# Values of all heads by seven products of quarters, in a stage of their own

## The chip, the cores and the metric

One core of one Trainium2 chip runs the whole kernel. The metric is the device time of one execution in microseconds. Three runs of the kernel before took 1961.91, 1963.91 and 1963.86 us, a median of 1963.86 us. Everything said of single instructions comes from one profiled execution of the same program.

## The reference

The model has two layers over 256 latent and 256 context tokens of width 2048. Layer 0 is bidirectional retention with 8 heads (q and k 256 wide, v and gate 512 wide per head), layer 1 is windowed attention. Cut to layer 0, on which the change bears:

```python
h = rms_norm(x) * (1 + scale) + shift            # scale, shift, gate from SiLU(c) @ ada_w
p = h @ w_in                                     # (512, 2048) @ (2048, 12288)
q, k, v, g = split(p)                            # per head: 256, 256, 512, 512 columns
q_l, k_l = rope_2d(q_l), rope_2d(k_l)            # latent tokens only, on a 4 x 64 grid
scores = (q @ k.T) / 16 * decay                  # gamma ** |i - j|, own gamma per direction
o = scores @ v                                   # latent tokens read context keys too
o = o * rsqrt(mean(o * o) + eps) * norm_gain
x = x + gate * ((o * silu(g)) @ w_out)
```

The modulation `SiLU(c) @ ada_w` gives shift, scale and gate for each layer and for two kinds of tokens, latent (c) and context (c_ctx). Layer 1's shift, scale and gate, and layer 0's gate, are needed only after the heads of layer 0. All matrices are float32.

## The kernel before

**Number format.** Every float32 operand of a large product is split into a high part (a rounded copy made by ScalarE, line 132 for weights, 116 for the rest) and a low part (the difference, made by VectorE, line 113). A product is then three matmuls, high x high, high x low, low x high: `mm3`, lines 137 to 142. A weight block is 256 rows by 512 columns, held as a tile of 128 x 1024 elements; `load_w` fetches it into one of three raw buffers over SP's queue and `split_w` makes the two parts, three buffers each.

**Start.** Tokens are loaded, normalised and modulated while TensorE already works on the queries and keys of heads 0 and 1 (`part0` and `part1`, lines 506 to 531). The products of head 0 stay in PSUM, those of head 1 are added up in SBUF (`qk1`).

**Head loop** (lines 899 to 925). Each head has three chunks of 512 weight columns: queries with keys, values, gate. A chunk is eight weight blocks. With tokens as the moving operand it is `gemm_ws`, with weights as the moving operand (values) `gemm_ts`; either way 4 x 16 calls of `mm3`, 192 matmuls of 512 columns. After each weight block a `hook` (line 727) issues a share of background work:

- one step of `sum_jobs` (line 311), which forms sums of quarters of the output projection in DRAM: a copy on ScalarE's queue, and an accumulating copy on POOL's queue held back by a tiny copy on POOL (`pin_t`);
- two steps of `ada_jobs` (line 694), the remaining modulation: a block of 128 x 512 of `adaB` is loaded and multiplied with the row of SiLU(c), once per kind of token, with a sum into one column (line 711, VectorE);
- one task of the head: moving queries and keys out with the rotation (`qk_evac`, line 739), a block of scores (`scores`, line 779), outputs, norm, and the parts of the gated branch (`parts`, line 836), whose sums POOL forms and which go to DRAM (`uB_d`) for the output projection.

The decay block of a head (`decays`, line 766) is two VectorE operations and a power of two on POOL (line 776); the rows come over ScalarE's queue.

**After the heads.** The output projection of layer 0 (lines 958 to 1154) is already computed by seven products of quarters: sums of weights come from DRAM (`wS_d`) or from VectorE (`comb`, line 974), and the accumulators are joined by ScalarE and VectorE (`merged`). Then layer 1 follows.

Instructions are written in program order, and a scheduler that knows dependencies and estimated durations sets the order on each engine; `tc.issue_after` holds instructions behind another one of the same engine. Each engine then works through its own order and waits on semaphores. A tile that shares its memory with an earlier one waits until that one is no longer used.

## Time and profile before

| what | value |
|---|---|
| three runs | 1961.91, 1963.91, 1963.86 us |
| span of the profiled execution, first to last instruction | 1959.6 us |
| its distance from the median of the runs | 4.3 us |
| TensorE busy | 1945.1 us, 99% |
| VectorE busy | 1350.5 us, 69% |
| ScalarE busy | 752.2 us, 38% |
| POOL busy | 481.6 us, 25% |
| bytes moved by DMA | 436.23 MB, mean 223 GB/s |
| start of the first chunk of the head loop, end of the last | about 148 and 1222 us |

An execution is described by the time from its first to its last instruction on the core. A row of instructions names line, engine, operation, output and inputs, count, busy time, the mean of one in nanoseconds, and the idle time ahead of it with what ended it. A row of a timeline gives the start, the duration and the instruction. The waits list for each engine who ended its idle time: total, times, longest. Matmuls overlap, so a busy TensorE is not yet one at its peak; distances between starts tell the rate.

### The profile page before, as it was taken

The numbers are of one execution on the slowest core, as the hardware profiler recorded it, in microseconds if no ns is written. First come the engines' busy times: TensorE is split into PE (matmuls) and PEld (weight loads), VectorE is DVE, ScalarE is ACT, GpSimd is POOL, SyncE is SP. The second block draws the span as 40 slices with busy tenths as digits, with TensorE's granted clock in tenths as the row PEclk, the third lists the DMA queues.
The fourth block names the chain that finished last, engine by engine and source line by source line (L and its number), as shares of the span: only waits on it lengthen the run. The fifth ranks groups of instructions, "written<-read, shape, count | busy, mean of one in ns | idle before, by whom it ended". The sixth has DMA issues, their size and how long they took to land.

```text
span 1959.6 us, 26859 instructions
## 1 busy us (share of the span) xinstructions
PE 1945.1 (99%) x9612; PEld 1612.6 (82%) x9612; DVE 1350.5 (69%) x2518; ACT 752.2 (38%) x1126; POOL 481.6 (25%) x389
## 2 busy tenths in 40 slices
PE   8999999999999999999999999999999999999999
PEld 4678888888888888888888888888888888888887
DVE  5566223788888888888565645877879746777764
ACT  4234223132222232232232334455555434766653
POOL 1218635525525526526300301100000100000000
PEclk9999999999999999999999999999999999999999
DMA  9965668898898998998755445677876324433365
GB/s 392 410 221 165 195 179 232 253 317 253 261 309 251 268 309 242 275 301 242 231 190 198 145 136 174 223 242 269 276 244 216 109 90 162 146 135 139 130 204 172
DMA packets 152039, 436.23 MB, mean 223 GB/s; under 512 B 18240, under 2 KB 37024, under 8 KB 146272
## 3 DMA queue, kind: packets, MB, share of 16 engines
q1 hardware_dynamic: 118976, 346.88, 50.6%
q0 software_dynamic: 10640, 34.87, 10.0%
q10 hardware_dynamic: 22288, 52.75, 7.8%
q8 instruction: 75, 1.23, 0.2%
q14 instruction: 60, 0.49, 0.1%
HBM read 416.04 MB, written 85.51 MB: 256 GB/s over the span
## 4 chain that ended last, share of the span: by engine, by line
PE 97%; DMA 1%; DVE 1%; issue 0%; ACT 0%; SPq 0%; DVEq 0%; ACTq 0%
PE acc L140 19%; PE acc L141 19%; PE acc L142 19%; PE acc L989 9%; PE acc L191 6%; PE acc L986 5%; PE acc L188 3%; PE pm L140 3%; PE pm L141 3%; PE pm L142 3%; PE acc L513 2%; PE pm L989 2%; PE pm L450 1%; PE pm L986 1%; PE pm L1307 1%; DMA rows<-gamT_d 1%
## 5 line engine op out<-in xcount | busy, mean ns | idle before, releaser
L132 ACT CAST wh<-wraw 128x1024 fp32r<-128x1024 f32 x415 | 435.2, 1052 | 848.5 <-PE acc L141 305.7
L113 DVE TENSOR_TENSOR wl<-wraw,wh 128x1024 fp32r<-128x1024 f32 x416 | 512.1, 1235 | 338.1 <-ACT wh L132 303.8
L140 PE MATMUL acc<-hT_h,wh 128*128 128x512 f32 x928 | 363.2, 391 | 1.0 <-DVE r_l L113 1.0
L141 PE MATMUL acc<-hl,wh 128*128 128x512 f32 x928 | 361.4, 389 | 0.0
L142 PE MATMUL acc<-hT_h,wl 128*128 128x512 f32 x928 | 361.2, 389 | 0.0
L711 DVE SCALAR_TENSOR_TENSOR ajunk<-abraw,crow 128x512 bf16<-128x512 f32 x448 | 344.2, 768 | 21.0 <-DMA abraw<-in_adaB 11.7
L142 PE MATMUL acc<-wh,hl 128*128 128x512 f32 x704 | 274.4, 390 | 0.0
L140 PE MATMUL acc<-wh,hT_h 128*128 128x512 f32 x576 | 224.7, 390 | 0.0
L141 PE MATMUL acc<-wl,hT_h 128*128 128x512 f32 x576 | 224.4, 390 | 0.0
L140 PEld LDWEIGHTS acc<-hT_h,wh 128*128 128x128 f32 x928 | 174.3, 188 | 38.0 <-DVE r_l L113 1.4
L142 PEld LDWEIGHTS acc<-hT_h,wl 128*128 128x128 f32 x928 | 174.2, 188 | 36.4
L141 PEld LDWEIGHTS acc<-hl,wh 128*128 128x128 f32 x928 | 174.4, 188 | 34.8
L241 POOL TENSOR_TENSOR rs<-ms,mhalf 128x4 f32<-128x4 f32 (+1 forms) x23 | 32.7, 1420 | 605.1 <-DVE ms L238 303.1
L776 POOL TENSOR_TENSOR dd<-two,dd 128x128 f32<-128x128 f32 x8 | 168.5, 21064 | 19.1 <-DVE dd L774 19.1
L142 PEld LDWEIGHTS acc<-wh,hl 128*128 128x128 f32 x704 | 132.2, 188 | 27.5
L322 POOL COPY pin_t<-wl 128x1 f32<-128x1 f32 x128 | 64.1, 500 | 317.5 <-DVE wl L113 313.2
L140 PEld LDWEIGHTS acc<-wh,hT_h 128*128 128x128 f32 x576 | 108.2, 188 | 23.1 <-issue 1.1
L141 PEld LDWEIGHTS acc<-wl,hT_h 128*128 128x128 f32 x576 | 108.2, 188 | 21.7
L324 POOL DMA_DIRECT2D wS_d<-in_wo x128 | 109.6, 872 | 11.2 <-issue 10.0
L843 POOL TENSOR_TENSOR ue<-sg 128x512 f32<-128x512 f32 x38 | 66.8, 1770 | 100.5 <-DVE sg L833 40.2
L829 POOL TENSOR_TENSOR ossq<-ossq,osq 128x512 f32<-128x512 f32 x24 | 35.3, 1470 | 185.7 <-ACT osq L823 185.0
L140 PE MATMUL acc<-wh,hl 128*128 128x512 f32 x192 | 75.4, 393 | 0.0
(282 smaller groups left out, 2915.1 us busy)
## 6 DMA issues: line engine op xcount, KB each, us to landing
wraw<-in_w SPq DMA_DIRECT2D x272, 512.0 KB, 4.2
abraw<-in_adaB SPq DMA_DIRECT2D x256, 256.0 KB, 5.5
wraw<-in_wo SPq DMA_DIRECT2D x80, 512.0 KB, 4.2
wS_d<-in_wo ACTq DMA_DIRECT2D x128, 256.0 KB, 5.2
wS_d<-in_wo POOLq DMA_DIRECT2D x128, 256.0 KB, 6.7
wraw<-wS_d SPq DMA_DIRECT2D x64, 512.0 KB, 4.5
araw<-in_adaS SPq DMA_DIRECT2D x28, 1024.0 KB, 11.5
wraw<-uB_d SPq DMA_DIRECT2D x20, 512.0 KB, 4.4
```

The costliest lines, as they stand in the source:

```text
L113: return nc.vector.tensor_tensor(out=out, in0=a, in1=hi.bitcast(F32), op=ALU.subtract)
L132: last_hi[0] = nc.scalar.copy(wh, raw).ins
L140: nc.tensor.matmul(ps, lhsT=ah, rhs=bh, start=start, stop=False, skip_group_check=skip)
L141: nc.tensor.matmul(ps, lhsT=ah, rhs=bl, start=False, stop=False, skip_group_check=skip)
L142: return nc.tensor.matmul(ps, lhsT=al, rhs=bh, start=False, stop=stop, skip_group_check=skip).ins
L191: nc.tensor.matmul(accs[j], lhsT=wk, rhs=h1(kb, s).rearrange("p a t -> p (a t)"), start=(kb == 0), stop=False)
L324: nc.gpsimd.dma_start(out=wS_d[i, r, q, x], in_=wo0_d[(*SUMS[i][1], r, q, x)], accum_op=ALU.add, max_dma_last_dim=4096)
L711: nc.vector.scalar_tensor_tensor(out=junk, in0=raw, scalar=1.0, in1=crow[:, t, q * 512:(q + 1) * 512], op0=ALU.mult, op1=ALU.mult, accum_o ...
L776: nc.gpsimd.tensor_tensor(out=dd, in0=two.to_broadcast([P, P]), in1=dd, op=ALU.pow)
L843: (nc.vector if now else nc.gpsimd).tensor_tensor(out=ue, in0=x, in1=y, op=op)
L986: last_pe[0] = nc.tensor.matmul(accs[j][:, 0:L], lhsT=wk, rhs=b[:, 0:L], start=False, stop=(kq == 3 and k == 3)).ins
L989: nc.tensor.matmul(accs[j], lhsT=wk, rhs=b, start=(kq == 0 and k == 0), stop=False)
```

## The change

The values of all heads leave the head loop. A stage ahead of it computes them in four pairs of heads. A pair is a product of 512 tokens by 2048 rows by 1024 columns, and each of the three sizes is halved: tokens into latent and context, rows into upper and lower half, columns into the two heads. Seven products of quarters (256 tokens, 1024 rows, 512 columns) replace eight. Sums of token quarters (`S`) are formed once, while TensorE computes the queries and keys of head 2; sums of weight quarters (`form`) are formed block by block; results are joined out of PSUM (`join`). All of these sums are VectorE's. Values go to DRAM (`v_d`) and are read back head by head (`v_load`). Queries and keys of heads 0 to 2 go through DRAM too (`qk_d`).

The order of the stage is written out in `VORDER`: each name is a product's accumulator group (X, Z, Y) and one of four row blocks; the position in the tuple says which sum of weights it takes.

```diff
+VORDER = ("X0 Z0 X1 Z1 X2 Z2 X3 Z3", "Y0 Z0 Y1 Z1 Y2 Z2 Z3 Y3", "X0 Y0 X1 Y1 X2 Y2 X3 Y3", "Y0 Y1 Y2 Y3")
...
-        t = strm.tile([P, 2, 512], F32, name="wraw", tag="wraw", bufs=3)
+        t = strm.tile([P, 2, 512], F32, name="wraw", tag="wraw", bufs=5)
...
+            for kp in range(4):
...
+                for j, x in enumerate(r):
+                    k, c = 2 * kp + 8 * (j % 2), half(j // 2)
+                    nc.vector.tensor_tensor(out=x, in0=hT_h[:, k:k + 2, c].bitcast(F32),
+                                            in1=hl[k // 2][:, :, c].bitcast(F32), op=ALU.add)
+                a11, a12, a21, a22 = r
+                for out, x, y, op in ((a22, a21, a22, ALU.add), (a21, a11, a21, ALU.subtract),
+                                      (a11, a22, a11, ALU.subtract), (a12, a12, a11, ALU.subtract)):
+                    nc.vector.tensor_tensor(out=out, in0=x, in1=y, op=op)
...
+                for i, x in enumerate((a22, a11, a21, a12)):
+                    split(S[i][:, ks, 0, :], S[i][:, ks, 1, :], x)
...
+            def form(self, g, m, kp):
+                raws, vt = self.raws, self.vt
+                if (g, m) == (0, "Z"):
+                    vt[kp] = ph.tile([P, 2, 512], F32, name="vt", tag=f"T{kp}")
+                    comb(vt[kp], raws[0, 12, kp], raws[0, 11, kp], ALU.subtract)
+                elif (g, m) == (1, "Y"):
+                    comb(vt[kp], raws[1, 22, kp], vt[kp], ALU.subtract)
+                elif (g, m) == (2, "Y"):
+                    comb(raws[2, 11, kp], vt[kp], raws[2, 11, kp], ALU.subtract)
+                    comb(vt[kp], raws[2, 21, kp], vt[kp], ALU.subtract)
...
+                for t in range(2):
+                    ts = slice(t * P, t * P + P)
+                    for k2 in range(2):
...
+                        mm3(acc[t], st, (wh[:, k2, :], wl[:, k2, :]),
+                            start=new and (kp, k2) == (0, 0), stop=last and k2 == 1, skip=True)
+                wide_hook(g)
+                if last:
+                    self.join(g, m)
...
+                if (g, m) == (0, "X"):
+                    self.q1 = self.tile("q1")
+                    each(lambda t, a: nc.scalar.copy(self.q1[:, t], a))
+                elif (g, m) == (0, "Z"):
+                    self.e = self.tile("e")
+                    each(lambda t, a: comb(self.e[:, t], a, self.q1[:, t], ALU.add))
...
+                elif (g, m) == (3, "Y"):
+                    each(lambda t, a: comb(self.q1[:, t], a, self.q1[:, t], ALU.add))
+                    self.store(1, 0, self.q1)
...
+        def wide_hook(g):
+            step_n[0] += 1
+            n = step_n[0]
+            if g != 2 and n % 2:
+                ada_step()
+            if n % 3 == 0:
+                next(sums, None)
...
+        for i in range(len(steps) + 3):
+            for what, back in (("load", 0), ("form", 1), ("parted", 2), ("mm", 3)):
```

The remaining modulation works on blocks of 128 x 1024 for 128 x 512; its raw blocks come through the same five buffers as the weights, and its steps are spread over the value stage (every other step, except in the third group) and the head loop (two per hook). What is left after the heads is issued at once (`ada_rest`). The sums of the output projection run at every third step of the value stage, at three of four hooks of the head loop, and for the rest at the hooks of the output projection itself.

```diff
+                for kb in range(KB):
+                    raw = load_raw(adaB_d[16 * part + kb, q].rearrange("p (a c) -> p a c", a=2))
+                    for t in range(ntk):
...
+                        nc.vector.scalar_tensor_tensor(
+                            out=junk, in0=flat, scalar=1.0, in1=crow[t],
+                            op0=ALU.mult, op1=ALU.mult, accum_out=asum[:, q, kb, t:t + 1])
```

The decay block is read from a table of powers in DRAM that is written once, each row shifted by one against the last. The rows of a head get a second buffer. The rotation's table shrinks to 4 row angles and 64 column angles, read with repetition.

```diff
+                nc.scalar.dma_start(out=skew_d.rearrange("h (r x) -> h r x", x=255),
+                                    in_=pow_d.unsqueeze(1).to_broadcast([H, P, 255]))
...
-            nc.vector.tensor_scalar(out=dd, in0=cst[:, C_T1:C_T1 + P], scalar1=lg2[:, h:h + 1],
-                                    scalar2=None, op0=ALU.mult)
-            nc.vector.scalar_tensor_tensor(out=dd, in0=cst[:, C_T2:C_T2 + P],
-                                           scalar=lg2[:, 8 + h:9 + h], in1=dd, op0=ALU.mult, op1=ALU.add)
-            nc.gpsimd.tensor_tensor(out=dd, in0=two.to_broadcast([P, P]), in1=dd, op=ALU.pow)
+            nc.scalar.dma_start(out=dd, in_=skew_d[h, 127:127 + P * 254].rearrange("(p x) -> p x", x=254)[:, 0:P])
```

In the head loop heads 0 to 2 keep only the gate chunk, with up to two tasks per hook; heads 3 to 6 have queries with keys and the gate; head 7 does its scores and its outputs inside its gate chunk, in an order written out (`plan`). The stores of the branch parts of heads 0 to 6 go from ScalarE's queue to POOL's. The gate's tile of a head is two tiles, in different memory for even and odd heads. The scratch memory for POOL's DMA descriptors is set to 4096 bytes.

```diff
         def hook():
+            state["n"] += 1
+            n = state["n"]
+            if n % 4 != 0:
+                next(sums, None)
+            if n > 2:
+                ada_step(2)
+            pump(rate[0])
...
-                    (nc.gpsimd if h == H - 2 else nc.scalar).dma_start(out=uB_d[m, h], in_=ue)
+                    (nc.scalar if h == H - 1 else nc.gpsimd).dma_start(out=uB_d[m, h], in_=ue)
...
+                if h:
+                    tasks.extend([e[0], outs[0], e[1], outs[1], nothing, v[0], outs[2], v[1], sc[0], sc[1],
+                                  outs[3], outs[4], sc[2], sc[3]])
...
+        plan = ([lambda: v_load(H - 1, 1), lambda: v_load(H - 1, 0)] + score_tasks(H - 1)[:1],
+                score_tasks(H - 1)[1:], outs[:1], outs[1:2] + [(M1, 2), (M1, 3)],
+                [(M1, 4), (M1, 5), (M1, 6), (M4, 0), (M4, 1)], outs[2:3] + [(M4, 5), (M4, 6), (M4, 2), (M4, 3)],
+                outs[3:] + [(M4, 4), (M1, 0), (M1, 1)])
```

374 lines of the change are left out of this document (237 added, 137 removed).

## The prediction

> **What bounds the kernel now.** I read the page's shares first, then who made TensorE wait, then stretches of the span, and last the single instructions.
>
> ```profile
> span 1959.6 us, 26859 instructions
> PE 1945.1 (99%) x9612; PEld 1612.6 (82%) x9612; DVE 1350.5 (69%) x2518; ACT 752.2 (38%) x1126; POOL 481.6 (25%) x389
> ```
>
> TensorE is busy 99% of the span. A matmul's end is modelled, so that share alone could hide gaps. The waits of TensorE say how many there are:
>
> ```profile
> PE pm L405 <- DMA x<-in_xT: 5.0, 1, 5.0
> PE acc L513 <- ACT hT_h L274: 3.0, 2, 1.8
> PE acc L140 <- DVE r_l L113: 1.0, 1, 1.0
> PE pm L450 <- DMA araw<-in_adaS: 0.5, 1, 0.5
> ```
>
> The four longest add up to 9.5 us, and all but 1.0 us of it lies at the start, ahead of the head loop. So the head loop has no idle that a change could win back; it gets shorter only if TensorE has less to do. What one matmul costs there is the distance between starts:
>
> ```profile
> 804.42 0.39 PE L140 MATMUL acc<-hT_h,wh 128*128 128x512 f32 x1
> 804.65 0.39 PE L141 MATMUL acc<-hl,wh 128*128 128x512 f32 x1
> 804.87 0.39 PE L142 MATMUL acc<-hT_h,wl 128*128 128x512 f32 x1
> 805.10 0.39 PE L140 MATMUL acc<-hT_h,wh 128*128 128x512 f32 x1
> 805.33 0.39 PE L141 MATMUL acc<-hl,wh 128*128 128x512 f32 x1
> ```
>
> Four distances take 0.91 us, so 0.2275 us each; the 0.39 us is latency.
>
> Who could take over as the bound is read from stretches of the span (columns: length, busy time of PE, PEld, DVE, ACT, POOL, granted clock, DMA share, GB/s):
>
> ```profile
> 400.00:900.00 500.00, 499.02 (x2269) 414.16 (x2268) 418.43 (x952) 137.54 (x200) 210.73 (x196) 1.00 0.91 278
> 1222.00:1310.00 88.00, 88.00 (x505) 76.94 (x504) 69.87 (x77) 43.31 (x59) 6.00 (x3) 1.00 0.68 227
> 1310.00:1534.00 224.00, 224.00 (x1286) 196.71 (x1285) 183.95 (x280) 123.78 (x180) 1.49 (x1) 1.00 0.71 242
> ```
>
> In the head loop VectorE is 84% busy and the DMA engines 91%, and TensorE does not stop. In the output projection of the first layer (the other two rows) VectorE is 79% and 82% busy, again with TensorE full. The granted clock is 1.00.
>
> **TensorE's term.** Before, the values of two heads cost 2 x 4 token blocks x 16 row blocks x 3 passes = 384 matmuls of 512 columns. After, a pair takes 28 steps (seven products of four steps each) of 2 token blocks x 2 row blocks x 3 passes: 336. Over four pairs that is 1344 for 1536, all of the 128x512 shape quoted: 192 fewer, 192 x 0.2275 = 43.7 us less. Queries and keys of head 2 are moved ahead, not removed; the transpose of the modulation row is moved to the start; scores and outputs keep their matmuls.
>
> [...]
>
> **What VectorE gets.** Prices are start to start, since an instruction's reported end overlaps the next start:
>
> ```profile
> 1249.88 3.49 DVE L113 TENSOR_TENSOR wl<-wraw,wh 128x1024 fp32r<-128x1024 f32 x3
> 1260.61 1.28 DVE L113 TENSOR_TENSOR hT_h<-wraw,hT_h 128x512 fp32r<-128x512 f32 x2
> 553.00 0.69 DVE L711 SCALAR_TENSOR_TENSOR ajunk<-abraw,crow 128x512 bf16<-128x512 f32 x1
> 553.61 0.08 DVE L711 DVE_READ_ACCUMULATOR ajunk<-abraw,crow 128x1 f32 x1
> 553.73 0.69 DVE L711 SCALAR_TENSOR_TENSOR ajunk<-abraw,crow 128x512 bf16<-128x512 f32 x1
> L113 DVE TENSOR_TENSOR wl<-wraw,wh 128x1024 fp32r<-128x1024 f32 x416 | 512.1, 1235 | 338.1 <-ACT wh L132 303.8
> ```
>
> Three wide subtractions in a row span 3.49 us, the last lasting 1.22: 1.135 us apart, for a mean duration of 1.235. Two narrow ones span 1.28 us: 0.60 apart. So 512 more elements cost 0.535 us. A narrow modulation sum takes 0.73 us start to start; the wide one, which the trace does not show, lies between 1.135 (a wide sum without the accumulator) and 1.46 (two narrow ones). I take 0.73 + 0.535 = 1.27, the nearest by shape. The 224 wide sums then take 284 us where 448 narrow ones took 327.
>
> By stage, VectorE against TensorE:
>
> 1. Chunk of head 2's queries and keys, 192 matmuls, 43.7 us. VectorE: 8 weight splits x 1.135 = 9.1; the four sums of token quarters, 32 adds and 16 split subtractions of 512 elements x 0.60 = 28.8; four ends of the start, 2.4. Together 40.3, 92%. What is late here is first needed a few products later, so I cost it at nothing; without that cover the loss is the excess alone.
> 2. Value stage, per pair 336 x 0.2275 = 76.4 us. VectorE: 28 splits and 16 weight sums, 44 x 1.135 = 49.9; ten joins out of the accumulators x 0.60 = 6.0; ten steps of modulation, 12.3 us (32 of 33 hold a sum). Together 68.2, 89%. ScalarE's 28 casts (row below) take 29 us.
> 3. Heads 0 to 2: one gate chunk each, 43.7 us, and 12.5 us of scores and outputs (36 matmuls of 512 columns, and 36 of 256 at 0.12 us, rows below): 56. VectorE: 8 splits 9.1, 16 modulation steps 19.7, and the head's own work (rotations, value splits, scores, outputs). That is worked out from the row 400 to 900: a head took 3 x 43.7 + 12.5 = 143.6 us, so 3.48 heads and 83.6 weight blocks lie in it, each with a split and four narrow sums, 1.135 + 4 x 0.73 = 4.06 us; 418.4 - 339.4 = 79 us are left, 22.7 a head, and 22 without the decay block. Together 51 us, 91%. Head 0 has no outputs to finish yet, 5 us less on both engines: 46 of 48, 96%.
> 4. Heads 3 to 6: two chunks, 100 us of TensorE; VectorE 18 + 39 + 22 = 79.
>
> ```profile
> L132 ACT CAST wh<-wraw 128x1024 fp32r<-128x1024 f32 x415 | 435.2, 1052 | 848.5 <-PE acc L141 305.7
> ...
> 783.21 0.28 PE L140 MATMUL pm<-r_h 128*128 128x256 f32 x1
> 783.33 0.28 PE L141 MATMUL pm<-r_l,r_h 128*128 128x256 f32 x1
> ```
>
> **Queues.** Moving the values costs transfers: 80 weight loads for 64, 16 stores of sums on ScalarE's queue and 16 loads back on SP, queries and keys of three heads out (ScalarE, and four on POOL) and in (SP), and the skewed rows: some 32 MB more. What the queues give:
>
> ```profile
> q1 hardware_dynamic: 118976, 346.88, 50.6%
> q0 software_dynamic: 10640, 34.87, 10.0%
> q10 hardware_dynamic: 22288, 52.75, 7.8%
> ```
>
> 346.88 MB in 50.6% of the span is 350 GB/s while busy; the accumulating queue 34.87 MB in 10.0%, 178 GB/s. In the value stage (306 us): 41.9 MB of weights, 10.5 of modulation, 8.4 of stores and 9.7 of copies at 350, 9.7 of accumulation at 178: 201 + 55 = 256 us, 84%. Heads 0 to 2, by the same prices for their 15 MB, come to about 50 of 56 us. Both lie under the 0.91 of the stretch 400 to 900, in which TensorE never waited. So the cost is nothing while the loads lead; if they do not, rival D.
>
> **Decays.** The power on POOL and its two VectorE operations go (L776: 8 x 21 us on POOL, and 0.6 us per head on VectorE), one small load on ScalarE's queue comes; the second buffer for the rows lets them come a head earlier:
>
> ```profile
> L776 POOL TENSOR_TENSOR dd<-two,dd 128x128 f32<-128x128 f32 x8 | 168.5, 21064 | 19.1 <-DVE dd L774 19.1
> DVE d L792 <- DMA rows<-gamT_d: 36.7, 7, 10.4
> ```
>
> These 36.7 us are VectorE's, none of it reached TensorE: worth nothing by itself, though it leaves VectorE freer. POOL takes on the stores of the branch parts (256 KB each, 4.1 us to landing, row under rival D); it was busy 25%.
>
> **New waits.** Each pair has five joins on VectorE, each waiting for the last matmul of a product. Behind a join in VectorE's order stand the sums and the split of the next steps, for which TensorE waits. The output projection has the same pattern: a step of 8 + 8 matmuls (about 2.8 us against 2.73 here), combined weights, joins, and it loses nothing at 79% to 82%. Not shown is 89%. A stall per join lies between 0 and, if all that may stand ahead comes late, 3.2 us (rival C). I take 0.2 us for each of the 20 joins, near the row of the same pattern: 4 us. The handover to head 0, whose tiles take the value stage's memory, and the last head, whose scores now share one chunk with its outputs (VectorE about 30 of 56 us), lie under a chunk each; bounds 0 and the landing of one 512 KB load (4.2 us, row under rival D) each; I take 1 each.
>
> **Sum**, against the profiled execution: 1959.6 - 43.7 + 4 + 2 = 1921.9 us of span. The runs shown have a median of 1963.86, 4.3 us above the span; so 1926 us.
>
> **Rivals.**
> B: VectorE becomes the bound where it is fullest. For: 89% to 96% is above anything in the trace. Against: it is less than full. Price: if the 16% that VectorE idled from 400 to 900 us are forced idle (waits for casts, transfers, products), the value stage needs 273 / 0.84 = 325 us instead of 306, the chunk ahead 48 for 44, heads 0 to 2 148 / 0.84 = 176 for 160: +39 us in full, 1959. At half that idle almost nothing is left (297, 44 and 161 us). I price it between, at 1942.
> C, slower: VectorE and TensorE go in lockstep at the joins. Two joins (1.2), two weight sums (2.27), a modulation sum (1.27) and the next split (1.135) stand in a row, 5.9 us, while TensorE has one step of 2.73 us prepared: 3.2 us lost at each of 20 joins, 64 us, 1984. It decides the sign from 2.2 us per join on. Against: weights can be split two steps ahead in three buffers, and the output projection shows no such loss. [...]
> D: modulation and weights share five raw buffers on SP's queue; a modulation block held by a late VectorE keeps weights from being fetched. The landing takes 4.2 us:
>
> ```profile
> wraw<-in_w SPq DMA_DIRECT2D x272, 512.0 KB, 4.2
> uB_d<-ue POOLq DMA_DIRECT2D x5, 256.0 KB, 4.1
> ```
>
> With a load late by half of that in one of four steps of the value stage it is 28 x 2.1 = 59 us at worst, and a fourth of that, 15 us, as its price: 1941. Against: five buffers are some five steps of lead, 13 us.
> E: the saved matmuls do nothing, because another limit sets the time: 1964. Against: the waits above.
>
> **How the numbers follow.** Forecast A (1918 to 1933) 0.62, B 0.18, C 0.08, D 0.08, E 0.04. The time is that of A, 1926. The low end is the fastest run less the whole saving, 1961.9 - 43.7 = 1918, and 2 us for unknown gains: 1916. The high end takes in most of B and D: 1956. About 0.2% (4 us) is what a measurement of this kernel can tell from no change. Faster: A, and nearly all of B and D: 0.87; same: E and the edge of B: 0.04; slower: C and the tail of D: 0.09.
>
> **What would show it.** Right: the value stage lasts 306 to 315 us with TensorE without waits and VectorE near 90%; the wide sum near 1.27 us apart; heads 0 to 2 some 56 us each; TensorE's matmuls 192 fewer. Wrong: TensorE's waits naming VectorE's weight split (B or C; in C right behind the joins) or raw loads (D) for more than 15 us in all.

## The result and the profile after

The changed kernel is slower: 2018.93 us (median of four, 2012.8 to 2021.72) against 1962.88 us before on the same chip (median of four), a ratio of 1.0282 with a 95% interval of 1.0265 to 1.03. The forecast was 1926. Of all the executions in this document one, of e15 below, took 6793.87 us; it is left out of that kernel's figures.

The head of the page of the changed kernel answers to the rows of before:

```profile
span 2011.0 us, 25977 instructions
PE 1935.6 (96%) x9420; PEld 1590.3 (79%) x9420; DVE 1487.8 (74%) x2250; ACT 820.9 (41%) x1214; POOL 374.6 (19%) x415
...
q1 hardware_dynamic: 106944, 371.59, 53.4%
q0 software_dynamic: 13360, 43.79, 11.1%
q10 hardware_dynamic: 23368, 56.95, 8.4%
```

TensorE has 9420 matmuls for 9612, so the 192 are gone. But its share fell from 99% to 96%, and VectorE, at 74%, is nowhere near full over the span. The longest of TensorE's waits (total, times, longest) say what came in:

```profile
PE acc L144 <- DVE t L947: 16.4, 6, 4.0
PE acc L145 <- DVE wl L114: 9.3, 8, 2.0
PE acc L146 <- DVE wl L114: 7.3, 3, 4.8
PE pm L145 <- DVE wl L114: 7.1, 7, 1.7
PE pm L1181 <- DVE x L1187: 5.8, 3, 3.1
PE pm L416 <- DMA x<-in_xT: 5.5, 1, 5.5
PE acc L144 <- ACT wh L136: 5.1, 3, 3.8
PE acc L1181 <- ACT wh L136: 4.3, 2, 2.8
PE pm L253 <- POOL ossq L1014: 3.2, 3, 1.6
```

All waits of TensorE, these and eight smaller groups, add up to 70.9 us; before they were 10.2. L947 is the rotation in a head's evacuation, L114 the split of a weight, L1187 a join of the output projection; the wait for `x` lies at the start, as before.

The waits are only half of it. This is TensorE's timeline around the first long pause:

```profile
160.58 0.39 PE L145 MATMUL acc<-hl,wh 128*128 128x512 f32 x1
165.79 0.79 PE L146 MATMUL acc<-hT_h,wl 128*128 128x512 f32 x1 [4.81 <-DVE wl L114]
166.38 0.63 PE L144 MATMUL acc<-hT_h,wh 128*128 128x512 f32 x1
166.80 0.63 PE L145 MATMUL acc<-hl,wh 128*128 128x512 f32 x1
...
171.07 0.56 PE L146 MATMUL acc<-hT_h,wl 128*128 128x512 f32 x1
171.47 0.39 PE L144 MATMUL acc<-hT_h,wh 128*128 128x512 f32 x1
```

Behind the pause the starts lie about 0.4275 us apart instead of 0.2275. From 165.79 to 171.07 there are 12 distances in 5.28 us where 2.73 would do: the pause of 4.81 us cost another 2.55 us. The granted clock of the changed kernel is 1.00 from 161.18 to 164.59, a stretch without a matmul, 0.50 from there to 171.42 and 1.00 behind, so the wide distances lie where half the clock is granted (shorter pauses: last section). The mean granted clock over the span is 0.986, against 0.999 before. As an estimate, if TensorE had had work all the time, that costs 2011.0 x 0.014 - 1959.6 x 0.001 = 26 us.

So the 51.4 us between the two spans are: -43.7 (matmuls saved) + 60.7 (more waiting) + 26 (clock) + 8 that neither view explains.

By stretches (length; busy time of PE, PEld, DVE, ACT, POOL; granted clock, DMA share, GB/s), cut at the start of the chunk of head 2's queries and keys, at the last copy of its results, at the last join of the values and at the last gate product of head 7:

```profile
148.00:201.00 53.00, 47.40 (x196) 38.12 (x195) 39.65 (x58) 20.34 (x29) 1.08 (x2) 0.94 0.40 129
201.00:530.00 329.00, 312.21 (x1344) 250.97 (x1343) 271.33 (x292) 127.90 (x130) 47.74 (x70) 0.99 0.81 245
530.00:1262.50 732.50, 703.38 (x3204) 582.37 (x3204) 563.83 (x915) 236.99 (x383) 239.99 (x246) 0.98 0.83 261
1262.50:2011.00 748.50, 733.87 (x3939) 628.35 (x3938) 531.16 (x808) 386.66 (x595) 68.37 (x83) 1.00 0.60 193
```

Without any waiting these would be 43.7, 306, 681 and 737 us: the first two from the prediction; the last is what lay behind the heads before (from 1222.8 to 1959.6); the third is the rest, 1959.6 - 43.7 - 148 - 43.7 - 306 - 736.8. The chunk lost 9 us, the value stage 23, the heads 51, the tail 12. All tables below use this cut.

### The profile page after: what moved, and what is told of

It is laid out like the page before. It is cut to its first block, busy times and chain, and to the rows that moved or that the text cites. A ratio compares the mean times of both kernels' runs of the same rounds, so it can differ in the third digit from the quotient of the medians.

```text
span 2011.0 us, 25977 instructions
## 1 busy us (share of the span) xinstructions
PE 1935.6 (96%) x9420; PEld 1590.3 (79%) x9420; DVE 1487.8 (74%) x2250; ACT 820.9 (41%) x1214; POOL 374.6 (19%) x415
## 3 DMA queue, kind: packets, MB, share of 16 engines
q1 hardware_dynamic: 106944, 371.59, 53.4%
## 5 line engine op out<-in xcount | busy, mean ns | idle before, releaser
L114 DVE TENSOR_TENSOR wl<-wraw,wh 128x1024 fp32r<-128x1024 f32 x416 | 512.4, 1237 | 248.0 <-ACT wh L136 236.8
L144 PE MATMUL acc<-hT_h,wh 128*128 128x512 f32 x928 | 371.4, 400 | 22.8 <-DVE t L947 16.4
L326 POOL COPY pin_t<-wl 128x1 f32<-128x1 f32 x128 | 91.0, 711 | 702.7 <-DVE wl L114 702.7
L678 DVE SCALAR_TENSOR_TENSOR wraw<-wraw,crow 128x1024 f32<-128x1024 f32 x128 | 169.3, 1329 | 14.2 <-DMA crow<-crow_d 11.3
L678 DVE SCALAR_TENSOR_TENSOR ajunk<-wraw,crow 128x1024 bf16<-128x1024 f32 x96 | 128.0, 1333 | 4.2 <-issue 3.0
L146 PE MATMUL acc<-wh,hl 128*128 128x512 f32 x320 | 125.3, 392 | 0.0
L136 ACT CAST wh<-vt 128x1024 fp32r<-128x1024 f32 x48 | 50.6, 1054 | 80.3 <-PE acc L146 35.6
L145 PE MATMUL acc<-wl,hT_h 128*128 128x512 f32 x192 | 75.8, 395 | 3.4 <-DVE wl L114 3.4
L144 PE MATMUL acc<-wh,hl 128*128 128x512 f32 x192 | 75.4, 393 | 0.0
L144 PE MATMUL pm<-r_h 128*128 128x512 f32 (+1 forms) x216 | 74.4, 344 | 1.0 <-DVE sg L1010 1.0
L144 PE MATMUL acc<-wh,hT_h 128*128 128x512 f32 x192 | 75.0, 392 | 0.2 <-ACT wh L136 0.2
L145 PE MATMUL acc<-wl,hl 128*128 128x512 f32 x192 | 74.9, 390 | 0.0
L145 PE MATMUL pm<-r_l,r_h 128*128 128x512 f32 (+1 forms) x216 | 74.1, 343 | 0.4 <-DVE r_l L114 0.4
## 6 DMA issues: line engine op xcount, KB each, us to landing
araw<-in_adaS SPq DMA_DIRECT2D x28, 1024.0 KB, 11.4
```

Of the source, the lines that this page charges most:

```text
L114: return nc.vector.tensor_tensor(out=out, in0=a, in1=hi.bitcast(F32), op=ALU.subtract)
L136: last_hi[0] = nc.scalar.copy(wh, raw).ins
L144: nc.tensor.matmul(ps, lhsT=ah, rhs=bh, start=start, stop=False, skip_group_check=skip)
L145: nc.tensor.matmul(ps, lhsT=ah, rhs=bl, start=False, stop=False, skip_group_check=skip)
L146: return nc.tensor.matmul(ps, lhsT=al, rhs=bh, start=False, stop=stop, skip_group_check=skip).ins
L326: pin = nc.gpsimd.tensor_copy(pin_t, last_wl[0][:, 0, 0:1].bitcast(F32)).ins
```

## The experiments

Where the text calls a kernel "the base", it is the changed kernel with six raw buffers and the values' reads behind the evacuation (e9). A "raw buffer" holds a block as it was loaded, ahead of its split; an "accumulating transfer" adds what it moves to what lies in DRAM. Code is shown shortened; some of the remarks behind # stand here alone. The executions of one of these kernels scatter more than those of before: four of the changed kernel span 9 us, four of e17 (below) 9 us, seven of e15 18 us. So single runs under some 20 us apart are told apart by their stages and waits, not by their totals. The stages are those of one profiled execution; it took 2012.8 us of the changed kernel, the fastest of its four, and 1982.2 of e15, the slowest of its seven.

An edit also lets the scheduler order the rest anew. By the traces, 253 instructions of VectorE lie in the value stage; against the changed kernel some 11% of them come in another order in e3, 19% in e4, 22% in e1 and 43% in e2. So these four runs show what an edit did together with its new order.

| kernel | time | chunk | values | heads | tail |
|---|---|---|---|---|---|
| forecast (1926 with 6 us of waits; the stages without any) | 1926 | 43.7 | 306 | 681 | 737 |
| changed | 2018.9 | 53.0 | 329.0 | 732.5 | 748.5 |
| e1 modulation without loads in the value stage | 2007.1 | 53.0 | 323.2 | 731.8 | 749.3 |
| e2 no weight sums in the value stage | 2016.1 | 51.8 | 310.2 | 744.0 | 760.0 |
| e3 modulation loads without sums | 2040.2 | 51.6 | 346.7 | 737.1 | 755.0 |
| e4 six raw buffers | 1987.2 | 50.0 | 317.6 | 715.7 | 754.1 |
| e5 values behind the evacuation | 1998.7 | 51.8 | 332.7 | 715.8 | 748.7 |
| e6 weight sums in the heads | 2020.2 | 53.4 | 330.0 | 748.1 | 738.9 |
| e7 later token sums, later head 0 | 2024.9 | 49.9 | 335.9 | 735.8 | 753.6 |
| e8 e4 to e7 together | 1984.1 | 47.3 | 322.0 | 725.4 | 739.5 |
| e9 base: e4 and e5 | 1976.7 | 52.3 | 317.4 | 705.5 | 751.7 |
| e10 base, modulation buffers apart | 2019.1 | 53.1 | 326.6 | 738.5 | 751.2 |
| e12 base, store through ScalarE | 1978.8 | 49.6 | 322.8 | 707.2 | 749.4 |
| e13 base, head 0 one step later | 1980.1 | 51.9 | 318.3 | 704.7 | 755.4 |
| e14 base, weight sums in the chunk | 1975.9 | 55.7 | 323.3 | 707.8 | 739.2 |
| e15 base, e12 to e14 | 1976.4 | 50.6 | 330.8 | 711.6 | 739.4 |
| e16 base, no accumulating transfer | 1942.2 | 51.6 | 307.9 | 694.4 | 738.1 |
| e17 base, weight sums spread | 1980.0 | 52.2 | 322.8 | 714.9 | 738.7 |
| e18 base, plain transfer instead | 1950.3 | 51.4 | 317.6 | 692.4 | 739.1 |

**Is VectorE full, or are the weights late?** (rivals B and D of the prediction: e1 to e4)

In e1 the value stage's modulation sums read a resident row instead of a raw block, so their loads are left out; in e3 the loads stay and the sums run over 8 columns; in e2 only the place of the weight sums changes.

```diff
 e1: +  flat = crow[t] if own else raw.rearrange("p a c -> p (a c)")     # own: value stage, no load
 e2: -            if n % 3 == 0:
     -                next(sums, None)                                   # value stage
     -            if n % 4 != 0:
     +            # every step of the head loop
                      next(sums, None)
 e3: +  cols = slice(0, 8 if in_values[0] else 1024)
     +  out=junk[:, cols], in0=flat[:, cols], scalar=1.0, in1=crow[t][:, cols],
 e4: -  t = strm.tile([P, 2, 512], F32, name="wraw", tag="wraw", bufs=5)
     +  t = strm.tile([P, 2, 512], F32, name="wraw", tag="wraw", bufs=6)
```

> Kernel after, but in the value stage the modulation sums multiply the resident row of SiLU(c) with itself: the same 40 wide sums on VectorE, none of their 20 loads through the raw buffers (a part of the modulation is left out). In the kernel after the value stage lasts 329 us (201 to 530) for 306 us of matmuls, with 17 us of TensorE's idle. Theory ring (weights come late because modulation shares the five raw buffers and holds them): stage about 312 us, TensorE idle under 5 us. Rival VectorE full: stage unchanged within 4 us. Rival DMA engines full: a little shorter, 320 to 326 us, as 10.5 of 80 MB go.

> Kernel after, but none of the sums of the output projection's weights in the value stage; they run at every hook of the head loop and the rest at the hooks of the output projection. 19 of 80 MB leave the value stage, and POOL's small copies that hold the weight buffers. Theory ring: stage about 325 us, little changed. Rival DMA engines full: stage about 312 us. Rival VectorE full: unchanged at 329 us. In all theories the time after the heads grows by some us, since 35 steps instead of 22 are left for it.

> Kernel after, but in the value stage each modulation sum works on 8 columns instead of 1024 (a part of the modulation is left out): loads and raw buffers as before, VectorE has 40 x 1.1 = 44 us less to do in the stage. Theory VectorE full: stage about 312 us. Theory ring: buffers are let go a little earlier, stage 322 to 329 us. DMA engines full: 329 us.

> Kernel after with six raw buffers for five (one buffer of the first modulation strips is given up for it, and most of the scratch memory of POOL's descriptors). Theory ring: value stage 318 to 324 us, and head loop shorter too, in all 10 to 30 us less. VectorE full or DMA engines full: value stage unchanged within 4 us.

e3 takes work off VectorE and the value stage gets longer, 346.7 for 329.0. None of the theories had that, and why it got longer stays open; it speaks against VectorE's load as the limit, and e16 below settles it. Taking traffic away shortens the stage: 323.2 without the modulation loads, 310.2 without the weight sums, both as the rival of full DMA engines had it (in e2 the time comes back in the heads and the tail). A sixth buffer shortens it to 317.6 with all the work in place and the heads by 17 us, as the theory of the ring, the shared buffers, had it. The sixth buffer's room comes from one buffer less for the modulation strips of the start (six for seven) and 1280 bytes of GpSimd's descriptor memory for 4096; these two sizes were not run alone. e10 has them too and gains nothing, which speaks against them but does not exclude them.

ScalarE's waits for a weight block, in its casts, show the lateness: in the kernel before,

```profile
ACT wh L132 <- DMA wraw<-in_w: 5.9, 2, 4.4
```

and in the changed kernel, with the waits of VectorE's sums of weights and of ScalarE's casts of values read back:

```profile
ACT wh L136 <- DMA wraw<-in_w: 116.7, 29, 9.5
ACT r_h L120 <- DMA wraw<-v_d: 55.5, 10, 10.1
DVE vt L117 <- DMA wraw<-in_w: 26.3, 17, 3.3
DVE wraw L117 <- DMA wraw<-in_w: 18.7, 12, 3.7
```

The median landing of a weight block hardly moved, 4.5 us for 4.2. What grew is how often a block isn't there when its cast is next. This row is a sign and no price: in e5 it is longer still, 135.2 us, with a shorter time, and in e16, the fastest version, 60.0 us are left.

**The values read back** (e5)

ScalarE's timeline in head 4 of the changed kernel, in the middle of the evacuation of queries and keys:

```profile
862.57 0.37 ACT L120 CAST r_h<-acc 128x256 fp32r<-128x256 f32 x1 [0.49 <-PE acc L146]
869.69 0.62 ACT L120 CAST r_h<-wraw 128x512 fp32r<-128x512 f32 x1 [6.75 <-DMA wraw<-v_d]
870.21 0.36 ACT L120 CAST r_h<-acc 128x256 fp32r<-128x256 f32 x1
```

A cast of the values waits 6.75 us for its load, the rest of the evacuation stands behind it, and TensorE, which needs the accumulators, pauses:

```profile
871.95 0.77 PE L144 MATMUL acc<-hT_h,wh 128*128 128x512 f32 x1 [3.98 <-DVE t L947]
```

```diff
+        def v_behind(h, i):
+            with tc.issue_after(last_ev[0]), tc.issue_after(last_ec[0]):   # last sum and last cast of the evacuation
+                v_load(h, i)
-                tasks.extend([lambda i=i: v_load(h, i) for i in (1, 0)] + score_tasks(h))
+                tasks.extend([lambda i=i: v_behind(h, i) for i in (1, 0)] + score_tasks(h))
```

> The changed kernel with one order altered: the two reads of a later head's values (v_load, heads 3 to 7), with their split on ScalarE and VectorE, are ordered behind the evacuation of that head's queries and keys, instead of wherever the planner finds room. Theory W (values read back are a new wait in front of the evacuation): in the changed kernel ScalarE's cast of the values waited 6.75 us at 869.69 for its transfer, the rest of the evacuation stood behind it, and TensorE paused for 2.4 to 4.0 us in each of heads 3 to 7 and ran slower right after; this run takes the waits of accumulator tiles for t (16.4 us in all) to near nothing and shortens the head stage from 732.5 to 710-722 us; the total falls to 1998-2010. Theory F (VectorE is full in the head stage, so a pause moves elsewhere): the head stage stays within 4 us of 732 and the waits come back at the scores that now get their values later.

As theory W had it in the stage: 732.5 to 715.8 us, total 1998.73. The value stage keeps its order of instructions, and nearly its length (332.7). The waits for t fell by half only, from 16.4 to 9.0 us, and not to near nothing: the rest stands behind a cast for a weight that came late, in the middle of the same evacuation (ScalarE's timeline of e5):

```profile
869.40 0.37 ACT L122 CAST r_h<-acc 128x256 fp32r<-128x256 f32 x1
872.26 1.04 ACT L138 CAST wh<-wraw 128x1024 fp32r<-128x1024 f32 x1 [2.49 <-DMA wraw<-in_w]
```

**The moved weight sums, the token sums, head 0** (e6, e7, e8)

In the tail three of TensorE's waits, 5.8 us, are for joins of the output projection (L1187 above), whose loads now share the transfers with the sums.

```diff
 e6: -            if n % 4 != 0:
     -                next(sums, None)
     +            next(sums, None)
     -                    next(sums, None)                              # in the output projection
 e7: +        stats, skip = stat_jobs(), [2]                            # first two calls do nothing
     -                    tasks.extend([lambda: (e[0](), e[1]()), lambda: (v[0](), v[1]()), nothing] + sc)
     +                    tasks.extend([nothing] * 5 + [e[0], e[1], nothing, v[0], v[1]] + sc)
```

> The changed kernel with the sums of weights for the output projection and the feed-forward part (sum_jobs) placed at every hook of the head loop instead of three of four, what is left finished ahead of the output projection, and none inside the output projection's own loop. Theory S (the sums that the change moved into the output projection cost there): a copy on GpSimd waited 6.85 us there, ScalarE's cast waited 8.81 us behind it, and TensorE's pauses of 1 to 3 us add up to some 10 us with what the slower clock adds; this run brings the tail from 748.5 to 735-742 us and costs the head stage up to 6 us. Theory N (the tail is longer for another reason, its own loads): the tail stays within 3 us of 748.5, and the head stage grows by the moved sums.

> The changed kernel with two places of its order altered: the token-quarter sums in the chunk of head 2's q and k begin two steps later (the last of them are finished right behind the chunk), and the reads of queries, keys and values of head 0 come at least two hooks later. Theory Q (in each place a load's wait stands on VectorE or ScalarE ahead of the split of a weight): the chunk falls from 53.0 to 44-48 us, and the pauses of 3.80 and 1.87 us in head 0 go, 4 to 8 us of the head stage; the total falls to 2000-2008. Theory R (the additions themselves are what delays the split, whatever they wait for): the chunk stays at 51-54 us or the time comes back at the start of the value stage, whose 329 us then grow.

> Six raw-weight buffers instead of five, together with the three edits of the runs beside it (values read behind the evacuation, sums of weights in the head loop alone, later token sums and later head 0). If the losses are separate and each has the cause named, they add up: chunk 44-48, value stage 312-320, head stage 695-715, tail 735-745, total 1935-1960, below the kernel before. If they share one limit (bytes per second or VectorE's total work), the total stays above 1970, and the value and head stages hold what the edits took from the others.

e6: the tail falls to 738.9 as theory S had it, and no pause for a join is left in it (one of 3.57 us at its start, for a weight's cast, stays); but the head stage takes 15.6 us more, where the theory allowed 6, so nothing is won. e7: the chunk falls by 3 us only, and a pause of 4.88 us appears at the start of the value stage; head 0's pause comes back later, 5.67 us at its outputs. That is theory R's outcome. e8, with everything, has each stage better than the changed kernel but the total at 1984, above the 1970 at which the losses were to be called one shared limit.

**Separate or shared buffers; the wide sums alone** (e9, e10, e11)

e11 also takes over the compact rotation table, which makes the room, and issues the sums one by one, where the kernel before issued them in pairs.

```diff
 e10: +    def load_m(src):                                              # modulation blocks
      +        t = strm.tile([P, 2, 512], F32, name="mraw", tag="mraw", bufs=2)
      -    wraw ... bufs=6
      +    wraw ... bufs=4
 e11 (on the kernel before):
      -                    for q in range(4):
      +                    for q in range(2):
      +                        raw = (top["pool"] if q else pb).tile([P, 2, 512], ...)
      -  in1=crow[:, t, q * 512:(q + 1) * 512]
      +  in1=crow[:, t, q * 1024:(q + 1) * 1024]
```

> Six shared raw buffers together with the values' reads behind the evacuation, and nothing else altered. Alone these two took 31.8 us and 20.2 us off the changed kernel. Theory A (two separate causes): they add up, 1963-1975, with the head stage at 700-708 us. Theory B (both relieve the same lateness of loads in the head stage): the second adds less than 8 us, 1979-1987, head stage 712-716 us.

> The same six buffers and the same order of the values' reads as the run beside it, but the buffers are split: four for the weights and the values read back, two of their own for the wide modulation loads, as the kernel before keeps the two apart. Theory O (the weights' loads are late because on SyncE's queue they stand behind a modulation load that waits for VectorE to finish an earlier sum of the same ring; in the changed kernel those waits come to 211.9 us): SyncE's queue waits for the wide sums fall, TensorE's waits for weights in the value and head stages fall below 15 us, and the time is 10-25 us under the run beside it. Theory L (what matters is how many buffers are ahead of the weights, not who holds them): with four in place of six for the weights the value stage goes back to 325-332 us and the time is 5-25 us above it.

> The kernel before with one part of the change alone: modulation sums of 1024 columns instead of 512, from two buffers of 4 KB that the modulation keeps for itself (four of 2 KB before), and the rotation's compact table, which makes the room for them. Values, decays and every other order stay as before. By the rows, a 512 sum takes 0.74 us start to start and a wide one 1.33 us with its read of the sum, so VectorE saves some 0.15 us in each pair, 230 x 0.15 = 35 us of busy time off the path. Theory P (the wide sums are harmless by themselves): within 0.4% of the kernel before, 1956-1968. Theory Q (a sum of 1.33 us, or a modulation load of 512 KB, in front of a weight's split is long enough to stop TensorE by itself): 10 to 30 us slower, with TensorE's waits naming VectorE's weight split in heads 1 to 6.

e9: 1976.7, between the two theories, with the head stage at 705.5 as theory A had it; the second edit still takes 10 us off the stage, so the causes are mostly separate. e10 was a miss for both theories, but for the value stage, which comes out at L's length (326.6): the time goes back to 2019.1, 42 us above e9 and beyond what L allowed, although the casts wait for weights less than in any other variant of the changed kernel, 21.5 us. The lateness has moved to the modulation: VectorE now stands in front of the splits waiting for its blocks (waits of VectorE in e10):

```profile
DVE ajunk L685 <- DMA mraw<-in_adaB: 43.1, 19, 5.6
DVE mraw L685 <- DMA mraw<-in_adaB: 29.4, 19, 3.1
```

In the base, with six buffers for all, these waits are 3.3 us together. e11 points the same way with the kernel before: 1971.13 against 1961.9, ratio 1.0041 (1.0027 to 1.0056), between the two theories. From two buffers of their own the wide sums, with the rest of that edit, cost 8 us; VectorE waits 65 us for their blocks, where the narrow sums waited 11.7, and TensorE pauses three times in the head loop, 6.9 us together.

**The three places that were left** (e12 to e15, on the base)

```diff
 e12: -            nc.gpsimd.dma_start(out=qk_d[1, :, j], in_=ends[j])
      +            nc.scalar.dma_start(out=qk_d[1, :, j], in_=ends[j])
 e13: -                    tasks.extend([lambda: (e[0](), e[1]()), lambda: (v[0](), v[1]()), nothing] + sc)
      +                    tasks.extend([nothing, nothing, e[0], e[1], v[0], v[1], nothing] + sc)   # two a step
 e14: +            next(sums, None)
      +            next(sums, None)                                      # each step of head 2's chunk
      -                    next(sums, None)                              # in the output projection
```

> Base: six shared raw buffers and the values read behind the evacuation (1976.72). Altered alone: the four stores of head 1's finished q and k go out through ScalarE's queue instead of GpSimd's. In the changed kernel VectorE's first token sum waited 8.18 us at the start of the chunk of head 2's q and k, for memory that the closed pool still stored from (stores landing 15.4 us after their issue). Theory H (that store is what it waits for): the wait falls by 5 us or more, the chunk from 52.3 to 44-47 us, the total to 1969-1973. Theory K (it waits for the other stores, of head 0's q and k or the decays): the chunk stays at 51-53 us and the total at 1975-1979.

> Same base. Altered alone: in head 0 the evacuation of queries and keys comes one step of the head loop later, two tasks a step from then on. The weight's cast at 542.70 stood behind a cast that waited 4.06 us for the read of the queries and keys and behind the evacuation's copies. Theory Q (order alone): the pauses of 3.87 and 1.87 us in head 0 go and the head stage falls from 705.5 to 696-700 us, total 1967-1972. Theory M (the work is needed by then anyway): the pause reappears within 60 us, at the scores or the output of head 0, total 1974-1982.

> Same base. Altered alone: two sums of weights in each step of the chunk of head 2's q and k (transfers busy 0.41 there), and none in the output projection. Theory S (the sums in the output projection keep its loads back and with them VectorE): the tail falls from 751.7 to 736-741 us; the chunk, with half of its transfer time free, grows by less than 3 us; total 1962-1968. Theory N (the tail's pauses have another cause): the tail stays above 747 us.

> The three edits of the runs beside it together on the same base. If each loss is a place of its own, as the theories above have it, 1946-1958, which is 0.2 to 0.8% below the kernel before; by the prediction's sum without any of these waits it would be 1926. If the pauses only move on, 1965-1980.

In the changed kernel VectorE's first token sum waits for memory of the pool that was just closed, out of which queries and keys are still being stored, and the split of the next weight stands behind it:

```profile
162.10 2.50 DVE L720 TENSOR_TENSOR vt<-hT_h,hl 128x512 f32<-128x512 f32 x4 [8.18 <-DMA qk_d<-qk0e]
164.51 1.22 DVE L114 TENSOR_TENSOR wl<-wraw,wh 128x1024 fp32r<-128x1024 f32 x1
```

In e12 the same sum waits less, but ScalarE now issues the four stores ahead of its casts:

```profile
156.15 2.94 ACT L138 CAST wh<-wraw 128x1024 fp32r<-128x1024 f32 x3 [7.42 <-DMA qk_d<-qk1e]
...
159.87 2.50 DVE L722 TENSOR_TENSOR vt<-hT_h,hl 128x512 f32<-128x512 f32 x4 [1.41 <-DMA qk_d<-qk1e]
```

The wait fell from 7.69 us in the base to 1.41, more than the 5 us of theory H. But the row of the changed kernel names head 0's stores (`qk0e`), which e12 left on their queue, and not the four of head 1 (`qk1e`) that it moved. So that stores out of the closed pool hold the sum is shown, and which of them decide is not. The chunk falls by 2.7 us only, since TensorE now pauses for 2.2 us in it behind a late cast. e13 moves head 0's pause from 543.80 to 544.07 us and makes the next one longer, 3.17 us for 1.87, as theory M had it. e14 brings the tail to 739.2 (theory S) and loses 3.4 us in the chunk and 5.9 in the value stage. e15: seven executions of 1964.51 to 1982.18 us, median 1976.4, against 1961.64, ratio 1.0058 (1.004 to 1.0077). The pauses move on.

**One shared limit?** (e16 to e18, on the base)

e16 leaves out the second half of every weight sum, which GpSimd's queue accumulates; the sums hold their first term alone. e18 makes that half a plain transfer on ScalarE's queue, with the same bytes; the sums hold their second term alone. e17 computes everything: two sums in each of the last six steps of head 2's chunk, five of six steps of the head loop, none in the output projection, and e12's store.

```diff
 e16: -  nc.gpsimd.dma_start(out=wS_d[i, r, q, x], in_=wo0_d[...], accum_op=ALU.add, max_dma_last_dim=4096)
      +  pass
 e18: +  nc.scalar.dma_start(out=wS_d[i, r, q, x], in_=wo0_d[...])
 e17: -            if n % 4 != 0:
      +            if n % 6 != 0:
```

> Base: six shared raw buffers and the values read behind the evacuation (1976.72). Left out of the computation: the second half of every sum of weights for the output projection (GpSimd's accumulating transfer), so the sums hold their first term alone; that takes GpSimd's queue, 43.79 MB and 11.4% of the transfer engines' time, off. Theory T (the loads come late because the value and head stages now ask for 0.81 to 0.85 of the transfer engines' time, so each edit so far only chose which load is late): chunk as before 52, value stage 308-312, head stage 690-697, tail 737-742, total 1938-1952. Theory P (single places of the order, one at a time, whatever the traffic): within 8 us of 1976.7 but for the tail, 1960-1972.

> Same base, with the sums of weights spread out: two in each of the last six steps of the chunk of head 2's q and k, five of six steps of the head loop, what is left ahead of the output projection, and none inside it; head 1's finished q and k are stored through ScalarE's queue. Under theory P: chunk 46-50, value stage 318-323, head stage 705-712, tail 738-741, total 1955-1970. Under theory T the tail's 12 us are given back by the stages that take the traffic, total 1970-1982.

> Base: six shared raw buffers and the values read behind the evacuation (1976.72). The second half of every sum of weights is a plain transfer of the same 256 KB through ScalarE's queue, in place of GpSimd's accumulating one; left out of the computation is the addition, so the sums hold their second term. Without the second half altogether the time was 1942.18. Theory T (any such traffic makes the loads late): 1958-1978, value stage 312-319, head stage 698-706. Theory G (it is GpSimd's accumulating queue: its descriptors, its reads of what it adds to, its longer landing): within 8 us of 1942, value stage 307-311, head stage 692-698.

e16 takes 1942.18 us, at theory T's figures in all four stages (307.9 for 308 to 312 in the value stage). The value and head stages in the stretches of the base:

```profile
200.30:517.70 317.40, 309.29 (x1343) 250.22 (x1342) 270.71 (x291) 128.04 (x130) 55.15 (x70) 1.00 0.82 253
517.70:1223.20 705.50, 691.90 (x3205) 574.58 (x3204) 563.15 (x915) 236.97 (x383) 242.48 (x246) 0.99 0.85 270
```

The same two stretches of e16:

```profile
199.60:507.50 307.90, 305.77 (x1344) 251.29 (x1343) 271.76 (x292) 128.19 (x130) 28.38 (x35) 1.00 0.70 234
507.50:1201.90 694.40, 687.86 (x3204) 573.16 (x3203) 556.44 (x915) 238.52 (x383) 182.90 (x174) 1.00 0.72 247
```

And of e18:

```profile
199.40:517.00 317.60, 310.29 (x1343) 253.21 (x1342) 271.43 (x291) 128.11 (x130) 27.46 (x35) 0.99 0.76 255
517.00:1209.40 692.40, 687.43 (x3205) 573.42 (x3204) 556.60 (x916) 238.38 (x383) 183.65 (x174) 1.00 0.80 275
```

In e16 VectorE is as busy in the value stage as in the base (271.76 for 270.71), and the stage takes 307.9: that is the 306 of the prediction, with 2.0 us of waits. No new order is in the way here: by the two traces, the 9420 matmuls of TensorE, the 2026 computing instructions of VectorE (reads of its accumulator aside) and the 1182 of ScalarE come in the same order in e16 as in the base. The 34.5 us between the two, about twice the widest scatter of one kernel, are thus what the accumulating transfers cost here. e17 wins the tail (738.7) and gives it back in the others: ratio 1.0096 (1.0073 to 1.0119). e18 falls between the two theories: the value stage goes back to the base's 317.6, as any traffic would have it (T), the heads and the tail stay where e16 had them (G). Of the 34.5 us that the accumulating transfers cost, 26.5 go with their kind and 8 stay with their bytes; 8 us is within the scatter of single runs, and in e18 some 12% of VectorE's instructions come in another order than in the base, so this split is an indication. The kind takes more of the transfer engines' time: with the accumulating transfers the base has 11.4% of the span on GpSimd's queue for e18's 1.4%, with the plain ones e18 has 13.7% on ScalarE's queue for 8.3%, so 10.0% of the span against 5.4% for the same bytes. Whether the kind costs by that, by its queue or by GpSimd's work for each (0.79 us) stays open. So does why the same 128 accumulating transfers did no harm before.

No version that computes everything beats the kernel before; the nearest with an interval is e15, 0.6% slower.

## Why the prediction was wrong, point by point

- **TensorE's term**, -43.7 us, was right: 192 matmuls fewer, and in e16 the value stage lasts 307.9 us, inside the 306 to 315 forecast.
- **Queues** is the step that failed: "So the cost is nothing while the loads lead; if they do not, rival D." The sum of the traffic was about right: 256 us of the value stage forecast, 0.81 x 329 = 266 measured. What failed is the conclusion from it: it compared mean shares (84% against a stretch at 0.91 without a pause) and took five buffers for enough lead. The casts' wait for weights went from 5.9 to 116.7 us. D had 0.08, and its price was a fourth of its worst case, 15 us; a sixth buffer alone returned 26 us against the fastest execution of the changed kernel and 32 against the median, and taking the accumulating transfers away from the base 34.5 more. That loads are late is shown; why the traffic makes them late at a lower mean share than before is not.
- **The sign of being wrong** pointed elsewhere: TensorE's waits name VectorE's weight split for 24 us and no raw load, which the prediction read as B or C. The late load stands a step further back, in the waits of ScalarE's casts and of VectorE's sums of weights.
- **"What is late here is first needed a few products later, so I cost it at nothing"** (chunk): the sums' results were indeed not needed yet, but the sums themselves stood ahead of a weight's split in VectorE's order while they waited 8.18 us for memory. The chunk lost 9 us, which is far more than "the excess alone".
- **The values' reads** were counted as bytes on SP's queue and as VectorE's splits, not as casts that wait in ScalarE's order. e5 puts them at 17 us of the head stage.
- **The handovers**, 1 us each: head 0's had two pauses, 3.80 and 1.87 us, and a slow clock behind them. e13 and e7 did not get rid of them.
- **The weight sums at the output projection's steps** stand in the description of the change, and the sum has no term for them. They cost 10 to 13 us of the tail (e6, e14, e17), and about as much or more wherever else they were put.
- **The clock** had no term: some 26 us by the estimate above.
- **New waits** at the joins, 4 us, and rivals B and C: e16 has the same joins and the same VectorE work, 88% of the value stage, and TensorE waits 2.0 us there; less VectorE work (e3) did not shorten the stage. So the fullness of VectorE and the joins were as harmless as the forecast had them, and VectorE's work was sized rightly: 273 us forecast for the stage, 271.3 busy. (One figure does not follow from its text: head 0's "46 of 48 us" takes 5 us off VectorE but 8 off TensorE; it bears on B's price alone.)
- **The wide sum** was right: 1.27 us forecast, and two in a row start 1.27 us apart in e11:

```profile
565.56 1.22 DVE L714 SCALAR_TENSOR_TENSOR ajunk<-abraw,crow 128x1024 bf16<-128x1024 f32 x1 [2.60 <-DMA abraw<-in_adaB]
...
566.83 1.22 DVE L714 SCALAR_TENSOR_TENSOR abraw<-abraw,crow 128x1024 f32<-128x1024 f32 x1
```

## What to carry to other kernels

Where TensorE is at 99%, price an edit not only by the work it takes away but by every wait that it puts ahead of a weight's cast or split in ScalarE's and VectorE's order: a load, memory of a closed pool, a store's issue. Count buffers against the longest lateness, not against the mean share of the queues, and price each pause of some 2 us or more with some 2 us on top for the slow clock behind it (an estimate: half of one slow stretch of 3.41 us is 1.7, and the first pause here cost 2.55). When single repairs only move the pauses, look for the traffic that they share, and take it away once to see what it costs.

## What the runs showed of the hardware

- The slow clock also follows pauses shorter than the 3.41 us of one of its stretches, and which ones depends on where they fall. In the trace of the changed kernel the granted clock is either 1.0 or 0.5, and it changes on a grid of 3.41 us: every slow stretch ahead of the span's end lasts 3.41 or 6.83 us. In e5 a pause of 1.79 us (496.8 to 498.5) lies within one stretch of that grid, and the next stretch runs at half clock; the matmuls behind the pause first start some 0.23 us apart, and from 500.03 on some 0.43. In e12 a pause of 2.41 us, which ended at 404.73, is parted between two stretches, 1.70 and 0.71 us, and no slow matmul follows. Rows as above, two of e5:

```profile
496.61:500.02 3.41, 1.62 (x7) 1.24 (x7) 3.41 (x6) 1.00 (x1) 0.00 (x0) 1.00 0.62 135
500.02:503.44 3.42, 3.42 (x10) 2.67 (x9) 3.42 (x4) 1.00 (x1) 0.00 (x0) 0.50 0.75 228
```

  And three of e12:

```profile
400.61:404.02 3.41, 1.71 (x8) 1.09 (x6) 2.30 (x3) 1.04 (x1) 0.00 (x0) 1.00 0.42 169
404.02:407.44 3.42, 2.71 (x12) 2.25 (x13) 3.42 (x5) 0.00 (x0) 0.96 (x2) 1.00 0.49 151
407.44:410.85 3.41, 3.41 (x17) 2.83 (x16) 3.41 (x4) 1.58 (x2) 0.00 (x0) 1.00 0.86 123
```

  So in these traces about half a stretch idle was often enough: 1.79 us in e5; in the changed kernel, from head 2's chunk on, each of the ten stretches at full clock with 2.00 us of idle time and more was followed by a slow one. The bound is not sharp: the stretch with 1.70 us in e12 was not followed by a slow one, and in the changed kernel the one at 676.59 with 1.55 us was and the one at 1287.58 with 1.64 was not.
- A copy of 128 x 1 on GpSimd, 0.44 us at 1274.28 in the tail of the changed kernel, is shown with 6.85 us ten us earlier:

```profile
1264.48 6.85 POOL L326 COPY pin_t<-wl 128x1 f32<-128x1 f32 x1 [6.02 <-DVE wl L114]
```

  VectorE ran back to back from 1260.79 to 1271.29; whether that held the copy, no run took apart.
